# Spread LayerNorm rows, one product for places and slot weights, ScalarE roots, banks per half: one block of retention, convolution and 32 experts

## The chip, the cores and the metric

The kernel runs on one core of one Trainium2 chip. The metric is the device time of one execution in microseconds (us). TensorE is written PE, VectorE DVE, ScalarE ACT, GpSimd POOL and SyncE, which here does nothing but issue DMAs, SP. Work reaches PE as matrix products in four-pass float32 (f32), in the rounded one-pass type fp32r, or in bf16.

## The reference

One post-norm layer over 256 tokens of width 1024 with a context prefix of 256 rows. A projection feeds two branches: retention with 8 heads (two heads make a pair p = 0..3 in the kernel) and a convolution with its own LayerNorm. Two sigmoid gates join them; a product with `w_mix_out`, a residual and LayerNorm 1 follow. Then each token goes to two of 32 experts, and LayerNorm 2 ends the layer. Every expert's weights are read, whatever the router chose.

```python
ret = jax.nn.silu(g) * _head_norm(o_ret)            # per head: (o - mean) * rsqrt(var + eps)
y_a = ret @ p['w_ret_out']
z = jax.nn.silu(_layernorm(_depthwise_conv(za * jax.nn.sigmoid(zb), ...), ...))
y_b = z @ p['w_conv_out'] + p['b_conv_out']
mix = (ga * y_a + gb * y_b) @ p['w_mix_out'] + p['b_mix_out']
h_lat = _layernorm(ALPHA * h_lat + gt_m * mix, p['ln1_g'], p['ln1_b'])
...
for e in range(N_EXPERTS):
    h = jax.nn.silu(t @ p['w_exp_gate'][e]) * (t @ p['w_exp_up'][e])
    y = y + combine[:, e:e + 1] * (h @ p['w_exp_down'][e])
h_lat = _layernorm(ALPHA * h_lat + gt_f * moe, p['ln2_g'], p['ln2_b'])
```

## The kernel before

**Order.** The kernel is recorded in the order in which it stands: `step` and `run_steps` keep a list of steps of the mixing sub-layer, `weave` inserts side steps at numbered places (`NPOS`, `APOS`, `TPOS`, `QPOS`), and each engine executes its own instructions in that order. A semaphore wait blocks everything behind it on its engine's queue. Because a product in fp32r keeps fewer bits, weights are split before use: `Slice.emit` lets ACT write the rounded half (`q[:, 0]`, L162) and DVE the rest (`q[:, 1]`, L163); `mm3` (L94 to L96) makes three fp32r products from the halves. The names are `qg` (gates), `qro` (`w_ret_out`), `qco` (`w_conv_out`), `qm` (`w_mix_out`).

**Last head pair and convolution norm.** While PE works on the first gates (`gate`, `gt`), `retain(3)` makes the retention outputs. Its `post` takes mean and variance (L684, L686) and gets the head norm's inverse root by integer arithmetic and Newton steps on DVE (`rstd`, L113 to L119). In the same loop `conv_rstd` starts the convolution's inverse root on DVE and gives its three Newton steps, twelve operations of 128x256, to POOL (L821 to L824). `post2` (L697, L700) scales and gates the heads on DVE alone. `ret_t` transposes them (`rt`, then `rT`, split by ACT and DVE), and `ret_out(3)` multiplies by `qro` into `ya`. `conv_norm` halves the normalisation between DVE and POOL (L829).

**The gate rows.** The adaLN sums `secs` (L918) are stored by POOL to a scratch row `arow` in DRAM (`rows_sum`). `rows_load` reads it back, spread over all partitions, into `tmp` and `gtf` (`bcast`, L78). Those two reads are issued by SP, which also issues all weight loads (`load`, L72). `conv_out(4..7)` (`yb`) then use `wco` tiles.

**LayerNorm 1 and router.** `mix_q` accumulates `mx`: the last accumulation of the second token tile goes in two halves of 256 columns that share a bank. `router_fold`, `router_mm` (`plog`) and `rank` pick the experts; `keep_clock(KC..)` adds idle products `clk`.

**Experts.** A list `plan` names 192 weight tiles of 1 MiB, six for each expert. `load_to` gives tile i the buffer class `slots[i]`: cycles of 18 tiles (`full`) up to slot `NCYC`, then 16 (`cyc`), then 12. A load waits until the buffer's last user is done. For each pair e0 = 0, 2, .. 30, `expert_pair` runs gate and up products (`gu`, L1375), `scatter` of the pair before (`y`, L1416), transposes (`ht`), `place`, which makes the slot-to-token matrix with two products and the slot weights with two more (`st`, L1450, L1452), and the down products (`dn`, L1485).

**LayerNorm rows.** The scale and shift rows of LN1 and LN2 lie on one partition (`lnv`). They are spread over 128 partitions by a product with a column of ones, in f32, 512 columns each: for LN1 at the end of pair 24 (`l1r`, L1645, used by L1647 to L1651 to start `yacc`), for LN2 at the end of pair 28 (`l2r`, L1657), behind the `tc.If` (L1628) that catches an overfull expert.

Of the kernel before, what the change touches and what calls it, by code (L numbers as in the profile page):

```python
# [17 lines left out]
D = 1024  # L18
# [13 lines left out]
NPOS, APOS, TPOS, QPOS, AHEAD = 7, 9, 7, 5, ()  # L32
# [4 lines left out]
NCYC = 130  # L37
CTX = 0, 0, 5, 6, 2
LNS = 20, 26, 24, 28
KC0, KC1, KC2, KC3, KC4 = 0, 2, 3, 4, 4  # L40
# [4 lines left out]
def tile_block(ctx, tc, a, out):  # L45
# [31 lines left out]
    def bcast(dst, src, n):  # L77
        nc.sync.dma_start(dst, bass.AP(tensor=src.tensor, offset=src.offset, ap=[[0, P], [1, n]]))  # L78
# [575 lines left out]
    def retain(p):  # L654
        box = {}

        def mm(_):
# [6 lines left out]
            if p == 3:  # L664
                conv_var()

        def post():
# [3 lines left out]
            more = []  # L671
            if p == 3:
                more = conv_rstd()
                for j in AHEAD:
                    more.insert(j, next_slice)

            def fill(i):
                if more:
                    more.pop(0)()
                elif i >= 2 and i % 3 != 1:  # L680
                    pop_conv(1)
# [5 lines left out]
            rstd(rs, mv[:, :, 1], 4, f"hn{p}", fill)  # L687
            while more:
                fill(0)
            box["n"] = mv, rs  # L690

        def post2():
            sr, (mv, rs) = srs[p], box["n"]
            for i in range(4):
                hh, t = divmod(i, 2)
                o = sr[:, 1, t, hh * NT:(hh + 1) * NT]
                V.tensor_scalar(o, box[hh][:, t], mv[:, i, 0:1], rs[:, i:i + 1], op0=ALU.subtract, op1=ALU.mult)  # L697
# [10 lines left out]

    last = []
# [104 lines left out]

    def conv_rstd():
        crs, ve, t = row1("crs"), row1("crsv"), row1("crst")
        nbox["rs"] = crs

        def newton():
# [6 lines left out]
        return rstd_ops(crs, nbox["var"], ve, t, 1.0 / D)[0:2] + [newton]  # L826
# [179 lines left out]
    def load_piece(which, o, n):  # L1006
        for e, t in which:
            load(t.rearrange("p k f -> p (k f)")[:, o:o + n], a["w_down"][e, 1, :, o:o + n])

    def down_view(t, cb):  # L1010

        t = t.rearrange("p k f -> p (k f)")
        return t.rearrange("p (k q f) -> p k q f", k=4, q=2) if cb == 0 else t.rearrange("p (q k f) -> p k q f", q=2, k=4)

    def load_to(n):
        while len(wts) < min(n, len(plan)):
# [5 lines left out]
            else:  # L1022
# [8 lines left out]
                t = down_view(t, r)  # L1031
# [6 lines left out]
    for p in range(3):  # L1038
# [10 lines left out]
          call(1, scores, 6), call(2, scores, 7), call(4, lambda: last.append(retain(3))), call(QPOS, step, lambda _: last[0]()),  # L1049
# [30 lines left out]
    def mix_q(cb, kq, box):  # L1080
        def mm(q):
            yT = ybox["y"]
            if kq == 0:
                box["ps"] = [acc(f"mx{cb}_{t}") for t in range(2)]
            box[kq] = q
            whole = slice(0, 512)
            order = [(kq, 0, whole), (kq, 1, whole)]
            if cb == 1 and kq >= 2:

                order = [(kq, 0, whole)]  # L1090
                if kq == 3:
                    order += [(n, 1, slice(256 * q, 256 * q + 256)) for q in range(2) for n in (2, 3)]
            for n, t, c in order:
                for kk in range(2):
                    k = 2 * n + kk
                    mm3(box["ps"][t][:, c], (yT[0][:, k, t * P:(t + 1) * P], yT[1][:, k, t * P:(t + 1) * P]),
                        (box[n][0][:, kk, c], box[n][1][:, kk, c]), k == 0, k == 7 and c.stop == 512)

        def post():
            if kq == 3:  # L1100
                r_ = [sb.tile([P, 512], F32, tag="b2", name=f"r{cb}_{t}", bufs=2) for t in range(2)]
                for t in range(2):
                    for q in range(2) if t and cb else (None,):
                        c = slice(0, 512) if q is None else slice(256 * q, 256 * q + 256)
                        cs = slice(512 * cb + c.start, 512 * cb + c.stop)
                        V.tensor_mul(r_[t][:, c], box["ps"][t][:, c], tmp[:, 1, cs])
                        V.tensor_add(xr[:, t, cs], xr[:, t, cs], r_[t][:, c])
                    for q in range(2):
# [649 lines left out]
```

## Time and profile before

| | us |
|---|---|
| median of 3 runs (974.23 to 975.60) | 975.26 |
| the profiled execution | 975.05 |
| its span on the core | 973.0 |
| PE busy | 928.3 (95%) |
| DVE busy | 518.5 (53%) |
| ACT busy | 313.2 (32%) |
| POOL busy | 100.6 (10%) |
| mean granted TensorE clock | 0.984 |

2.05 us of the profiled execution lie outside the span. The page gives shares over the whole span; the stages differ. Up to about 487 us PE works on the mixing sub-layer, from 500 us on the experts, and the last 13 us are LayerNorm 2. DMA moves 292.8 MB from HBM, two thirds of it expert weights. In a timeline row stand the start, the duration, engine, line, operation, out<-in, and in brackets the idle time ahead with the instruction that ended it. Successive products overlap, so the distance between two starts, not the duration, is the pace.

### The profile page before, as it was taken

What the parts mean: (1) busy time and instruction counts of PE and PEld (TensorE: products, weight loads), DVE (VectorE), ACT (ScalarE), POOL (GpSimd) and SP (SyncE); (2) the same over time, 40 slices, a digit from 0 to 9 for tenths busy, and PEclk for the clock granted to TensorE, in tenths of its full rate; (3) what the DMA queues carried; (4) which work ended last, traced back from release to release, by engine and by line L of the source; (5) the groups of instructions that cost most, each with busy time, mean ns of one, the idle gap of its engine ahead of it and who ended that gap; (6) DMA issues with size and microseconds to landing.
All of it is one profiled execution on the core that took longest, in us unless ns stands there. A gap on an engine that the chain in (4) does not pass through costs nothing. (4 is left out here: it accounts for less than half of the span.)

```text
span 973.0 us, 15303 instructions
## 1 busy us (share of the span) xinstructions
PE 928.3 (95%) x6327; PEld 688.2 (71%) x6327; DVE 518.5 (53%) x1000; ACT 313.2 (32%) x459; POOL 100.6 (10%) x114
## 2 busy tenths in 40 slices
PE   8999999999999999898999999999999999999994
PEld 6898798888789888798877656665555555535552
DVE  3598979878978976874844213121222222142126
ACT  2468444445345343653433102121111111112110
POOL 1020400400300213504100000000000000000001
PEclk9999999999999999999999999999999999989987
DMA  9967225634255176548998999999999999999971
GB/s 352 419 234 252 83 93 194 256 141 184 114 205 224 44 303 228 206 155 313 369 366 314 423 421 421 420 420 421 420 420 422 420 420 420 420 421 420 419 302 44
DMA packets 48744, 294.92 MB, mean 303 GB/s; under 512 B 10304, under 2 KB 10352, under 8 KB 14368
## 3 DMA queue, kind: packets, MB, share of 16 engines
q1 hardware_dynamic: 47888, 293.22, 75.3%
q8 instruction: 51, 0.84, 0.3%
q0 software_dynamic: 784, 0.70, 0.3%
q14 instruction: 21, 0.17, 0.0%
HBM read 292.77 MB, written 1.12 MB: 302 GB/s over the span
## 5 line engine op out<-in xcount | busy, mean ns | idle before, releaser
L1375 PE MATMUL gu<-wgate,xe 128*64 128x256 f32 x1024 | 123.0, 391 | 0.7 <-DMA wgate<-in_w_exp_gate_dram 0.5
L1375 PE MATMUL gu<-wup,xe 128*64 128x256 f32 x1024 | 117.7, 380 | 3.4 <-DMA wup<-in_w_exp_up_dram 3.4
L1485 PE MATMUL dn<-wdown,hT 128*64 128x512 f32 (+1 forms) x528 | 117.1, 583 | 3.6 <-DVE hT L1443 2.5
L335 DVE SCALAR_TENSOR_TENSOR slab<-zp,taps,slab 128x256 f32<-128x256 f32 x232 | 109.2, 525 | 0.0
L1375 PEld LDWEIGHTS gu<-wgate,xe 128*64 128x64 f32 x1024 | 74.6, 140 | 45.3 <-issue 9.9
L1381 DVE TENSOR_TENSOR h<-h,gu 128x256 f32<-128x256 f32 x32 | 13.5, 421 | 171.9 <-ACT h L1380 171.9
L1375 PEld LDWEIGHTS gu<-wup,xe 128*64 128x64 f32 x1024 | 73.9, 137 | 41.6 <-DMA wup<-in_w_exp_up_dram 6.6
L1485 PEld LDWEIGHTS dn<-wdown,hT 128*64 128x64 f32 x528 | 40.3, 137 | 68.2 <-issue 58.6
L1380 ACT ACTIVATE h<-gu 128x256 f32<-128x256 f32 x32 | 12.3, 384 | 205.5 <-PE gu L1375 205.5
L1498 DVE SCALAR_TENSOR_TENSOR dl<-dn,ws,ohq 128x512 fp32r<-128x512 f32 x30 | 22.5, 751 | 94.0 <-ACT ohq L1497 94.0
L1497 ACT ACTIVATE ohq<-dn,ws 128x512 fp32r<-128x512 f32 x30 | 20.6, 687 | 130.1 <-PE dn L1485 127.4
L1355 PEld LDWEIGHTS ga<-ohq,xh 128*128 128x128 f32 x224 | 27.9, 188 | 15.9 <-issue 11.1
L95 PE MATMUL ya<-rT,qro 128*128 128x256 f32 x128 | 36.7, 287 | 2.5 <-DVE rT L726 2.5
L75 POOL DMA_DIRECT2D lnv<-in_ln_g_dram x2 | 1.0, 521 | 367.3 <-PE dn L1485 302.8
L96 PE MATMUL glu<-ulh,qz 128*128 128x256 f32 x128 | 36.4, 284 | 1.9 <-DVE qz L163 1.9
L96 PE MATMUL gt<-ulh,qg 128*128 128x256 f32 x128 | 36.2, 283 | 1.9 <-DVE qg L163 1.9
L94 PE MATMUL glu<-ulh,qz 128*128 128x256 f32 x128 | 37.2, 291 | 0.2 <-ACT qz L162 0.2
L96 PE MATMUL ya<-rT,qro 128*128 128x256 f32 x128 | 36.6, 286 | 0.8 <-DVE qro L163 0.8
L1362 DVE TENSOR_SCALAR xe<-ga,cf 128x256 f32<-128x256 f32 x32 | 17.4, 544 | 37.2 <-ACT xe L1365 36.3
L94 PE MATMUL ya<-rT,qro 128*128 128x256 f32 x128 | 37.0, 289 | 0.0
L1355 PE MATMUL ga<-ohq,xh 128*128 128x256 f32 x224 | 33.6, 293 | 3.4 <-DVE dl L1498 3.4
L94 PE MATMUL gt<-ulh,qg 128*128 128x256 f32 x128 | 36.7, 287 | 0.0
(461 smaller groups left out, 2151.4 us busy)
## 6 DMA issues: line engine op xcount, KB each, us to landing
wgate<-in_w_exp_gate_dram SPq DMA_DIRECT2D x64, 1024.0 KB, 19.8
wup<-in_w_exp_up_dram SPq DMA_DIRECT2D x64, 1024.0 KB, 19.8
wdown<-in_w_down_dram SPq DMA_DIRECT2D x62, 1024.0 KB, 19.8
wa<-in_w_ada_r_dram SPq DMA_DIRECT2D x16, 1024.0 KB, 4.9
wa<-in_w_ada_m_dram SPq DMA_DIRECT2D x8, 1024.0 KB, 14.5
wro<-in_w_ret_out_dram SPq DMA_DIRECT2D x8, 1024.0 KB, 6.9
wg<-in_w_gates_dram SPq DMA_DIRECT2D x8, 1024.0 KB, 7.2
wz<-in_w_glu_dram SPq DMA_DIRECT2D x5, 1024.0 KB, 13.1
```

The source lines that it names most:

```text
L94: T.matmul(ps, st[0], mv[0], start=start, stop=False)
L95: T.matmul(ps, st[0], mv[1], start=False, stop=False)
L96: T.matmul(ps, st[1], mv[0], start=False, stop=stop)
L335: V.scalar_tensor_tensor(dst, zp[:, ct, j:j + NT], taps[:, ct, j:j + 1], ac[ct], op0=ALU.mult, op1=ALU.add)
L1355: T.matmul(ps[:, kk], halves[k // 4][:, s, t, P * (k % 4):P * (k % 4) + P], ohr[:, t], start=(t == 0 and s == 0), stop=(t == 1 and s == 1))
L1362: V.tensor_scalar(xe[c][:, k], ps[:, kk], fsc[:, k:k + 1], fsh[:, k:k + 1], op0=ALU.mult, op1=ALU.add)
L1375: T.matmul(ps[64 * hf:64 * hf + 64, j], xe[c][:, k, CAP * i:CAP * i + CAP], w[:, k % 4, NT * hf:NT * hf + NT], start=start, stop=stop)
L1380: S.activation(h, ps[:, 0], AF.Silu)
L1381: V.tensor_mul(h, h, ps[:, 1])
L1485: T.matmul(ps[64 * x:64 * x + 64], hT[x][:, ch % 2, 64 * (ch // 2):64 * (ch // 2) + 64], w, start=(ch == 0), stop=(ch == 3))
L1497: S.activation(dh, ps, AF.Copy, scale=ws)
L1498: V.scalar_tensor_tensor(dl, ps, ws, dh.bitcast(F32), op0=ALU.mult, op1=ALU.subtract)
```

## The change

1. **Rows.** `l1r` and `l2r` go. `pieces(n)` makes eight pieces of 256 columns of a LayerNorm's two rows; for each, ACT rounds the row piece and DVE takes the rest, and two fp32r products spread both halves into one bank. `row()` runs one piece after each `hidden` and after each half of the down products: LN1's in pairs 20 and 22, LN2's in pairs 24 and 26. `lnv` is loaded at the end of pair 18, `yacc` begins there too, and `NCYC` falls from 130 to 112.
2. **Places.** `iw` holds the identity and, beside it, the slot weights of all experts. Two products of 192 columns replace the two of 128 and two of 4; DVE then adds the pair's weights out of the bank.
3. **Roots.** For the last head pair and the convolution, ACT's square root and DVE's reciprocal with one Newton step replace integer start and Newton steps (`rstd_pair`, `conv_root`, `conv_rstd`). `post2` follows at once, with two of its four scalings on ACT (in all pairs), and `ret_t` moves one place ahead.
4. **Banks.** The two halves of the last `mx` get a bank each.
5. **Reads of `arow`** are issued by POOL instead of SP.
6. **Small.** `least` is made in `router_fold`; `og` goes to POOL, and `ig4` no longer needs it; the `KC` counts fall; the last two experts' down weights get a DRAM array of their own.

```diff
-NPOS, APOS, TPOS, QPOS, AHEAD = 7, 9, 7, 5, ()
+NPOS, APOS, TPOS = 7, 9, 6
-NCYC = 130
+NCYC = 112
-LNS = 20, 26, 24, 28
-KC0, KC1, KC2, KC3, KC4 = 0, 2, 3, 4, 4
+LNS = 18, 20, 22, 24
+KC0, KC1, KC2, KC3, KC4 = 0, 0, 2, 2, 3
...
+                rstd_pair(rs, mv[:, :, 1], "hn3", 4, conv_root)
+            V.scalar_tensor_tensor(nb, mv[:, :, 0], -1.0, rs, op0=ALU.mult, op1=ALU.mult)
+            box["n"] = mv, rs, nb
+            if p == 3:
+                post2()
+                conv_rstd()
...
+            for i in (1, 0, 3, 2):
+                if t:
+                    S.activation(o, box[hh][:, t], AF.Identity, scale=rs[:, i:i + 1], bias=nb[:, i:i + 1])
...
     def conv_rstd():
-            for _ in range(3):
-                G.tensor_mul(t, crs, crs)
-                G.tensor_mul(t, t, ve)
-                G.tensor_scalar(t, t, -0.5, 1.5, op0=ALU.mult, op1=ALU.add)
-                G.tensor_mul(crs, crs, t)
+        V.reciprocal(crs, crs)
+        V.tensor_mul(t, crs, crs)
+        V.tensor_mul(t, t, nbox["h"])
+        V.scalar_tensor_tensor(crs, t, 1.5, crs, op0=ALU.add, op1=ALU.mult)
...
-        bcast(tmp[:, 1], arow[0], D)
-        bcast(gtf, arow[1], D)
+        bcast(tmp[:, 1], arow[0], D, nc.gpsimd)
+        bcast(gtf, arow[1], D, nc.gpsimd)
...
-                box["ps"] = [acc(f"mx{cb}_{t}") for t in range(2)]
+                box["ps"] = [(t, c, n, acc(f"mx{cb}_{t}_{c}")) for t in range(2)
+                             for c, n in (((0, 256), (256, 256)) if t and cb else ((0, 512),))]
...
-                T.matmul(pt[:, t * P:(t + 1) * P], oh[t], identr, start=True, stop=True)
-            for t in range(2):
-                T.matmul(pt[:, NT:NT + 4], oh[t], Wr[:, t, e0 // 2], start=(t == 0), stop=(t == 1))
+                T.matmul(pw[:, t], oh[t], iw[:, t], start=True, stop=True)
...
+    def pieces(n):
+        def split(i, c):
+            row = lnv[0:1, i, 256 * c:256 * c + 256]
+            h = box["h"] = sb.tile([P, 2, 256], F32R, tag="rope", name=f"lnh{n}{i}{c}", bufs=1)
+            S.activation(h[0:1, 0], row, AF.Copy)
+            V.tensor_sub(h[0:1, 1], row, h[0:1, 0].bitcast(F32))
+        def use(i, c):
+            ps = bank("mi", f"ln{n}{i}{c}")[:, 0:256]
+            for j in range(2):
+                T.matmul(ps, oner[0:1], box["h"][0:1, j], start=(j == 0), stop=(j == 1))
+            if n:
+                S.activation(lnv[:, i, cs], ps, AF.Copy)
+                return
...
-        if e0 == LNS[3]:
-            for i in range(4):
-                ps = bank("mi", f"l2r{i}")
-                cs = slice(512 * (i % 2), 512 * (i % 2) + 512)
-                T.matmul(ps, onef[0:1], lnv[0:1, i // 2, cs], start=True, stop=True)
-                S.activation(lnv[:, i // 2, cs], ps, AF.Copy)
+        for n in range(2):
+            if e0 == LNS[2 * n]:
+                rows.extend(pieces(n))
+                rows.pop(0)()
```

SP's queue before the second half of the gates' end, at the reads of `arow` (`wco` and `wm` are tiles of `w_conv_out` and `w_mix_out`; `wgate` is an expert's). Before:

```order
L78 DMA tmp<-in_b_mix_out_dram 128x1024
L78 DMA tmp<-arow 128x1024
L78 DMA gtf<-arow 128x1024
L72 DMA wco_4326<-in_w_conv_out_dram 128x2048
L72 DMA wco_4387<-in_w_conv_out_dram 128x2048
L72 DMA wgate_0_4452<-in_w_exp_gate_dram 128x2048
L72 DMA wm_0_4454<-in_w_mix_out_dram 128x2048
```

The same place after; the two reads now stand on POOL's queue, behind the stores of `arow` and ahead of a product of gate and `yaT`.

```order
L78 DMA tmp<-in_b_mix_out_dram 128x1024
L72 DMA wco_4324<-in_w_conv_out_dram 128x2048
L72 DMA wco_4385<-in_w_conv_out_dram 128x2048
L72 DMA wgate_0_4450<-in_w_exp_gate_dram 128x2048
L72 DMA wm_0_4452<-in_w_mix_out_dram 128x2048
```

No weight load stands behind a read of `arow` any more. DVE in the stage of the last head pair, from the last small Newton operation on (`sr` are the scaled heads, `crs` the convolution's inverse root, `rT` the rest of the transposed heads). Before:

```order
L119 SCALAR_TENSOR_TENSOR rs_3645<-hn3t,rs_3645 128x4
L163 TENSOR_TENSOR qg_2_3686<-wg_1_3684,qg_2_3686 128x1024
L697 TENSOR_SCALAR sr_3336<-o_3623,mv_3644,rs_3645 128x256 x2
L697 TENSOR_SCALAR sr_3336<-o_3632,mv_3644,rs_3645 128x256 x2
L700 TENSOR_TENSOR sr_3336<-sr_3336 128x2x256 x2
L163 TENSOR_TENSOR qg_3_3722<-wg_1_3684,qg_3_3722 128x1024
L163 TENSOR_TENSOR qro_0_3753<-wro_0_3751,qro_0_3753 128x1024
L726 TENSOR_TENSOR rT_3782<-rt_0_3783,rT_3782 128x512
L829 TENSOR_TENSOR zp<-zp,crs 128x4x256
```

And after:

```order
L686 SCALAR_TENSOR_TENSOR nb_3651<-mv_3649,rs_3650 128x4
L700 TENSOR_SCALAR sr_3338<-o_3625,mv_3649,rs_3650 128x256
L700 TENSOR_SCALAR sr_3338<-o_3634,mv_3649,rs_3650 128x256
L703 TENSOR_TENSOR sr_3338<-sr_3338 128x2x256 x2
L824 RECIPROCAL crs<-crs 128x256
L825 TENSOR_TENSOR crst<-crs 128x256
L826 TENSOR_TENSOR crst<-crst,crsh 128x256
L827 SCALAR_TENSOR_TENSOR crs<-crst,crs 128x256
L165 TENSOR_TENSOR qg_2_3690<-wg_1_3688,qg_2_3690 128x1024
L165 TENSOR_TENSOR qg_3_3720<-wg_1_3688,qg_3_3720 128x1024
L727 TENSOR_TENSOR rT_3749<-rt_0_3750,rT_3749 128x512
```

The split of `qg_2` for the third pair of gates now stands behind the scaled heads and the whole inverse root; two scalings have left DVE. PE behind pair 28, where the `tc.If` ends. Before:

```order
L1628 UNCONDITIONAL_BRANCH
L1657 MATMUL l2r_7667<-lnv,oner 128x512
L1657 MATMUL l2r_7670<-lnv,oner 128x512
L1657 MATMUL l2r_7673<-lnv,oner 128x512
L1657 MATMUL l2r_7676<-lnv,oner 128x512
L1375 MATMUL gu_7679<-wgate_0_7358,xe_7181 64x256 x8
```

And after, and in a second fence where such products now stand (`ln`, between the experts of pair 20):

```order
L1682 UNCONDITIONAL_BRANCH
L1381 MATMUL gu_7750<-wgate_0_7445,xe_7245 64x256 x8
L1381 MATMUL gu_7750<-wgate_1_7447,xe_7245 64x256 x8
```

```order
L1381 MATMUL gu_6658<-wup_0_6439,xe_6458 64x256 x8
L1381 MATMUL gu_6658<-wup_1_6441,xe_6458 64x256 x8
L1642 MATMUL ln_6694<-lnh_6645,oner 128x256 x2
L1381 MATMUL gu_6702<-wgate_0_6443,xe_6458 64x256 x8
L1381 MATMUL gu_6702<-wgate_1_6445,xe_6458 64x256 x8
```

One piece of a row, two short products, follows the gate and up products of each expert, and the last pair's products follow the branch directly.

## Rows read from the trace of the kernel before

**Rows 1.** Windows: from:to, length, busy per engine, PEclk, DMA share, GB/s
```profile
404.00:407.00 3.00, 3.00 (x20) 3.00 (x19) 0.51 (x2) 0.67 (x3) 0.00 (x0) 0.66 0.81 330
435.00:440.00 5.00, 5.00 (x45) 5.00 (x44) 2.25 (x5) 2.84 (x4) 0.84 (x2) 1.00 0.00 0
525.00:530.00 5.00, 5.00 (x26) 2.89 (x24) 0.75 (x1) 0.69 (x1) 0.00 (x0) 1.00 0.31 128
900.00:925.00 25.00, 23.01 (x155) 12.74 (x152) 3.85 (x9) 2.85 (x6) 0.00 (x0) 1.00 1.01 419
```
**Rows 2.** DMA issues of the page: KB each, median us to landing
```profile
wgate<-in_w_exp_gate_dram SPq DMA_DIRECT2D x64, 1024.0 KB, 19.8
```
**Rows 3.** Waits of PE, 780 to 860 us: total, times, longest
```profile
PE gu L1375 <- DMA wup<-in_w_exp_up_dram: 3.4, 7, 0.7
```
**Rows 4.** Waits of SP's queue, 440 to 560 us
```profile
SPq L78 <- DMA arow<-secs: 19.2, 2, 18.9
SPq L72 <- PE dn L1485: 18.8, 3, 9.0
```
**Rows 5.** Timeline of SP, 420 to 456 us
```profile
441.19 0.33 SPq L78 DMA_DIRECT2D tmp<-arow  x1
...
442.37 0.86 SPq L72 DMA_DIRECT2D wco<-in_w_conv_out_dram  x2
```
**Rows 6.** Timeline of PE at the second half of the convolution's output
```profile
452.45 0.39 PE L94 MATMUL yb<-zh,qco 128*128 128x256 f32 x1 [2.63 <-ACT qco L162]
...
453.71 0.50 PE L96 MATMUL yb<-zh,qco 128*128 128x256 f32 x1 [0.76 <-DVE qco L163]
...
457.36 0.28 PE L95 MATMUL yb<-zl,qco 128*128 128x256 f32 x1
457.48 0.28 PE L96 MATMUL yb<-zh,qco 128*128 128x256 f32 x1
```
**Rows 7.** Timeline of PE, last head pair, 388 to 416 us
```profile
391.17 0.39 PE L96 MATMUL gt<-ulh,qg 128*128 128x256 f32 x1 [0.26 <-DVE qg L163]
...
396.30 0.39 PE L96 MATMUL gt<-ulh,qg 128*128 128x256 f32 x1 [1.60 <-DVE qg L163]
...
403.22 0.58 PE L95 MATMUL ya<-rT,qro 128*128 128x256 f32 x1 [2.54 <-DVE rT L726]
```
**Rows 8.** Timeline of DVE in the same stage
```profile
385.27 0.36 DVE L686 BATCH_NORM_AGGREGATE mv<-st 128x2 f32<-128x6 f32 x4
...
391.03 1.89 DVE L697 TENSOR_SCALAR sr<-o,mv,rs 128x256 f32<-128x256 f32 x4
392.85 1.73 DVE L700 TENSOR_TENSOR sr<-sr 128x512 f32<-128x512 f32 x2
...
403.09 1.21 DVE L163 TENSOR_TENSOR qro<-wro,qro 128x1024 fp32r<-128x1024 f32 x1
```
**Rows 9.** Reciprocals of DVE by form: busy us, mean ns
```profile
L254 DVE RECIPROCAL l<-l 128x16 f32<-128x16 f32 x1 | 0.3, 253 | 0.0
...
L1220 DVE RECIPROCAL dv<-dv 128x2 f32<-128x2 f32 x1 | 0.2, 166 | 0.1
```
**Rows 10.** Timeline of DVE at the last product of the mixing
```profile
490.25 0.42 DVE L1106 TENSOR_TENSOR r<-mx,tmp 128x256 f32<-128x256 f32 x1 [0.60 <-PE mx L96]
```
**Rows 11.** Timeline of PE, ends of pairs 24 and 28 and the last pair
```profile
865.42 6.04 PE L1375 MATMUL gu<-wgate,xe 128*64 128x256 f32 x32
871.30 3.62 PE L1375 MATMUL gu<-wup,xe 128*64 128x256 f32 x32
...
922.90 5.40 PE L1657 MATMUL l2r<-lnv,oner 1*128 1x512 f32 x8 [1.81 <-DVEq L1628]
928.24 5.36 PE L1375 MATMUL gu<-wgate,xe 128*64 128x256 f32 x32
...
948.45 5.96 PE L1485 MATMUL dn<-wdown,hT 128*64 128x512 f32 x32
```
**Rows 12.** Timeline of SP, 915 to 946 us: the last six loads
```profile
917.68 12.79 SPq L72 DMA_DIRECT2D wdown<-in_w_down_dram  x6
```

More of the change, by code (lines that the diff above doesn't have):

```diff
@@ L670, in post @@
             rs = sb.tile([P, 4], F32, tag="rs", name=f"rs{p}", bufs=2)
[L671 to L675, printed above, removed]
+            nb = sb.tile([P, 4], F32, tag="nb", name=f"nb{p}", bufs=1)
             def fill(i):
-                if more:
-                    more.pop(0)()
-                elif i >= 2 and i % 3 != 1:
+                if i >= 2 and i % 3 != 1:
                     pop_conv(1)
@@ L1007, in load_piece @@
         for e, t in which:
[L1008 to L1013, printed above, removed]
+            load(t.rearrange("p k f -> p (k f)")[:, o:o + n], a["w_down_last"][e - (NE - 2), :, o:o + n])
     def load_to(n):
@@ L1101, in post @@
                 r_ = [sb.tile([P, 512], F32, tag="b2", name=f"r{cb}_{t}", bufs=2) for t in range(2)]
-                for t in range(2):
[L1103 to L1108, printed above, removed]
-                        V.bn_stats(st1[:, t, 2 * cb + q], xr[:, t, 512 * cb + 256 * q:512 * cb + 256 * q + 256])
+                for t, c, w, ps in box["ps"]:
+                    cs = slice(512 * cb + c, 512 * cb + c + w)
+                    V.tensor_mul(r_[t][:, c:c + w], ps[:, 0:w], tmp[:, 1, cs])
+                    V.tensor_add(xr[:, t, cs], xr[:, t, cs], r_[t][:, c:c + w])
+                    if c or w == 512:
+                        for q in (2 * cb, 2 * cb + 1):
+                            V.bn_stats(st1[:, t, q], xr[:, t, 256 * q:256 * q + 256])
         key = (cb, kq // 2)
@@ L1482, in product @@
                 for x in range(2):
-                    w = wts[e0 + x, "down", cb][:, ch]
-                    w = w[:, cs.start // 256] if cs.stop - cs.start == 256 else w
+                    w = wts[e0 + x, "down", cb]
+                    w = w[:, cs.start // 256, ch] if last and cb else w[:, ch]
                     T.matmul(ps[64 * x:64 * x + 64], hT[x][:, ch % 2, 64 * (ch // 2):64 * (ch // 2) + 64],
@@ L1617, in tile_block, with one_, go, row @@
     lnv = yacc = None
+    def pieces(n):
+        box = {}
+        def split(i, c):
[4 more added lines that the diff above has]
+        def use(i, c):
+            cs = slice(256 * c, 256 * c + 256)
+            ps = bank("mi", f"ln{n}{i}{c}")[:, 0:256]
[4 more added lines that the diff above has]
+                return
+            r, o = divmod(c, 2)
+            for t in range(2):
+                if i == 0:
+                    V.scalar_tensor_tensor(yacc[:, t, cs].rearrange("p (q k) -> p k q", k=4),
+                                           ps.rearrange("p (q k) -> p k q", k=4), ALPHA,
+                                           xn[:, t, r, :, 64 * o:64 * o + 64], op0=ALU.mult, op1=ALU.mult)
+                else:
+                    V.scalar_tensor_tensor(yacc[:, t, cs], ps, ALPHA, yacc[:, t, cs], op0=ALU.mult, op1=ALU.add)
+        todo = [(i, c) for i in range(2) for c in range(4)]
+        def one_(j):
+            def go():
+                if j:
+                    use(*todo[j - 1])
+                if j < len(todo):
+                    split(*todo[j])
+            return go
+        return [one_(j) for j in range(len(todo) + 1)]
+    def row():
+        if rows:
+            rows.pop(0)()
+    rows = []
     for e0 in range(0, NE, 2):
```

115 lines of the change are left out of this document (58 added, 57 removed).

## The prediction

> **What bounds the kernel now.** I read the page's shares first, then windows of each stage, then the waits ahead of PE and of SP's queue, and the timelines where they stand. The page says PE is busy 95% of the span, which would make PE the bound everywhere. The windows say otherwise. In the expert stage the DMA share is 1.01 at 419 GB/s and PE has two us of 25 to spare [rows 1]; the 25 us windows from 550 to 925 all show 1.01 or 1.02. A tile of 1 MiB takes 1.0486 MB / 420 GB/s = 2.5 us, a pair of experts 12 x 2.5 = 30 us. PE needs 23.01 / 25 x 30 = 27.6 us for it, so it has about 2.4 us a pair, and from 780 us on it waits for weights, in short pieces [rows 3]. There the kernel ends when the weight stream ends, plus what PE does behind the last tile. PE is the bound in two places only: ahead of the stream, and behind it.
>
> The stream does not start by itself. At 525 to 530 us the DMA share is 0.31 [rows 1], and SP waits 18.8 us in three waits for PE's first down products, which hold the buffers [rows 4]. So whatever brings PE sooner to the experts moves the whole stream by as much, and whatever makes PE faster inside it is worth nothing. That is the frame for each part.
>
> **Reads of `arow` (b).** SP waits 18.9 us for `arow` [rows 4] and issues its read at 441.19; behind it stand `wco` (issued 442.37 [rows 5]), an expert tile and `w_mix_out`. In 435 to 440 us no byte moves [rows 1]. PE then stands still for 2.63 us and again for 0.76 us, waiting for the halves of `wco`, and runs slowly for a while [rows 6]. From 452.45 - 2.63 = 449.82 to 457.36 it starts 19 products; at the pace of the last two rows, 0.12 us each, they are 2.3 us. Lost: 7.54 - 2.3 = 5.3 us. After the change SP goes on to `wco` at once. Its buffers come free as the gates' weights are split; I put the last of these splits at about 436 us, and two tiles need 5 us of the idle DMA, so they land some 9 us ahead of need. I take the whole 5.3; the lower end is 4, if the splits themselves on ACT and DVE are late. POOL waits for its own store instead, for a landing of perhaps 2 us; behind that stand the product with `yaT` and the one for `tmp`, needed only when the convolution output is done. Nothing else queues there.
>
> **Last head pair and roots (a).** Before, PE loses 0.26 + 1.60 + 2.54 us [rows 7], and then the granted clock is 0.66 in 404 to 407 us [rows 1]: at its lower level for 0.34 / 0.5 x 3 = 2 us, which costs 1.0. With the bit before 404, some 5.6 us. After, the split of `qg_2` stands behind more work on DVE. Means end at 385.27 + 0.36 = 385.6 [rows 8]; nine small operations, with ACT's roots between, take about 1.9; two scalings instead of four, half of 1.89 [rows 8], 0.95; the gating 1.73 [rows 8]: 390.2. Then the reciprocal of 128x256, which the trace does not have. The rows have 253 ns for 16 columns and 166 for two [rows 9], 6.2 ns for each more, so 166 + 254 x 6.2 = 1.74 us. Three operations of 128x256 at 0.42 [rows 10] and the split at 1.21 [rows 8] end at 394.4. PE is out of weights at 391.17 - 0.26 = 390.9 [rows 7]: a wait of 3.5 us, where before there were 0.26. Behind it the weights and transposes are ahead of PE, since the twelve POOL operations and ACT's late transposes are gone, and the waits of 1.60 and 2.54 fall away. The 2.54 us wait was followed by the lower clock and the one of 1.60 was not, so I charge the long one with 1.2 us more: 4.7 us in all, a gain of 0.9. Upper end 2.3, if the clock holds; lower end -1.6, if the wait for `rT` stays as well (4.7 + 2.5 against 5.6). The two table loads that ACT now needs lie in idle time of ACT ahead of the roots and behind them. The scalings given to ACT in the other pairs lie beside a PE that is busy, at nothing.
>
> A word on the reciprocal: the rows show 6.2 ns a column where the other small operations show far less. The Trainium skill, "VectorE: DVE Perf Modes", section "First, the fixed hardware budget", says that the reciprocal is an iterative divide with a repeat count of 8; if that is eight cycles of the 0.96 GHz clock that its "Specifications" give, an estimate by that page is 256 x 8 / 0.96 + 150 ns = 2.3 us. By it the sum below would be 0.5 us higher; the rows speak for the shorter price.
>
> **Banks, `og`, clock products (c).** DVE waits 0.60 us for the whole last `mx`, though its first half is done by then [rows 10]: with its own bank that goes. `og` on POOL takes one operation of about 0.2 (the size of the small one in [rows 9]) off DVE's chain to the router, and the fewer idle products let the last `plog` start some 0.25 sooner. Sum 1.0; ends 0.3 (another wait is behind each) and 1.5.
>
> **Up to the stream:** 5.3 + 0.9 + 1.0 = 7.2 us, carried to the end by the frame above.
>
> **Inside the stream.** A piece is two products of 256 columns, 0.24 us at the pace of [rows 6]; four a pair are 1.0 us of the 2.4 spare. Its split needs ACT and DVE for one-partition operations, both idle there. `yacc` takes over the buffer of a weight tile and may hold DVE until PE has used that tile, which delays the down products of one pair by 1 us at most: in the spare time too. The places' product, two of 192 columns for two of 128 and two of 4, is nothing either way. The ring shrinks earlier (16 tiles instead of 18 from slot 112): with 19.8 us from issue to landing [rows 2], 8 tiles are under way, so PE may be 8 tiles, 20 us, late before a load is held up. I price the whole at 0; without the cover it would be 16 x 0.24 = 4 us.
>
> **Behind the stream (d).** Before, the LN2 rows take 5.40 us between the last pairs, and the products behind them run at 5.36 us instead of 3.62 [rows 11]: 7.1 us on the path to the last down products at 948.45. The LN1 rows cost PE the like (6.04 against 3.62, [rows 11]), which it carries as lateness into the last pairs. After, neither stands there. PE alone would reach the down products 7.1 us sooner or more. The stream allows more: the last six loads start at 917.68 [rows 12], so the first lands at 937.5, the second at 940.0, and four half tiles of 1.25 us by 945.0; the down products need the second, 8.4 us sooner than now. I take 7.5. Lower end 5.5, if PE has to wait for that tile and drops its clock (1.74, the difference above); upper end 8.4.
>
> **Sum.** 975.05 - 7.2 - 7.5 = 960.35 for the profiled execution; the span is 973.0, and the 2.05 us around it stay. The median of the runs lies 0.2 above that execution: **960.5**. By the ends of the terms: 975.25 - (4 - 1.6 + 0.3 + 5.5) = 967 to 975.25 - (5.3 + 2.3 + 1.5 + 8.4) = 957.7.
>
> **The rivals.**
> *The stream is not moved.* If DMA itself, not PE, is late between 441 and 525 us, the 7.2 us do not arrive; only the tail is gained: 975.25 - 7.5 = 967.7. Against it: the idle DMA at 435 to 440 and 525 to 530 [rows 1], together some 8 us.
> *The path does not open.* `wco` waits for its buffers instead of `arow`, or POOL's read lands late: b falls to about 1 and the time is 965.
> *The pieces cost clock (slower).* Both old row products, on one partition, had the clock fall behind them [rows 11]. If each of the 16 pieces did so at the 1.74 us of LN2, a pair of PE would take 4 x (0.24 + 1.74) = 7.9 us more with 2.4 to spare: late by 4 x 5.5 = 22 after pair 26, less 2 x 2.4 regained, 17 behind the stream where before it was 7.5; with 7.2 gained earlier, +2.5, and as the loads would then be held up too, some 979. It decides from about 1.5 us a piece. Against it: a piece is 0.24 us between full products, the old ones were 5 to 7 us in one stretch with waits.
> *Nothing measurable*, if two of these meet and the tail gives little: about 975.
>
> **How the numbers follow.** Forecast as worked out, 957 to 964.5: 0.62. Head stage or tail at its lower end, or `wco` late, 964.5 to 968: 0.15. Stream not moved, 967.7: 0.08. Better than 957, by waits that I don't see go: 0.07. Nothing: 0.03. Slower by the pieces: 0.05. A measurement of this kernel tells about 0.2%, 2 us, from no change. Faster 0.92, same 0.03, slower 0.05. The range 954 to 968 takes in the ends of the terms and the rival of the unmoved stream.
>
> **What would show it.** b: `wco` issued by 436 us, `yb` without a wait ahead, the DMA busy at 435 to 440. a: one wait of 3 to 4 us for `qg`, none for `rT`, a reciprocal of 1.7 us. c: the DVE wait for `mx` gone. Stream: DMA share 1.01 from about 523 us on. d: down products of the last pair at about 933 to 934 us (948.45 - 14.7), with wider gaps of PE at full clock in pairs 26 to 30. Wrong would be a clock under 1 in pairs 20 to 26, a DMA share under 1 after slot 112 (some 745 us), or a new wait of SP ahead of `wco`.

## The result and the profile after

| | before | after |
|---|---|---|
| median of 4 runs, us | 975.10 | 962.61 |
| lowest to highest, us | 974.23 to 975.60 | 961.64 to 963.80 |
| profiled execution, its span, us | 975.05, 973.0 | 962.05, 960.2 |
| mean granted TensorE clock | 0.984 | 0.991 |

After over before is 0.9873 (95% interval 0.9856 to 0.9891): 12.5 us less, where 960.5 us, 14.8 less, was forecast and 954 to 968 was the range. Time and range were right, but the terms were not, and two of their misses cancel.

To see where the time went I compare the starts of the same PE product in both traces.

| PE reaches | before | after | gained by then |
|---|---|---|---|
| a product of `qp`, after the decay rates | 89.38 | 90.54 | -1.2 |
| the `yb` product that waits for `zl`, after the roots | 417.73 | 418.31 | -0.6 |
| the 19th `yb` product of the second half | 457.21 | 452.38 | 4.8 |
| `ppos`, the router's end | 498.41 | 493.34 | 5.1 |
| first `gu` of the experts | 503.35 | 500.07 | 3.3 |
| places of pair 0 | 521.43 | 518.14 | 3.3 |
| places of pair 18 | 761.19 | 757.95 | 3.2 |
| last `y` ahead of the last half tiles | 954.34 | 941.85 | 12.5 |

The reads of `arow` gave what was forecast. SP's timeline after: `wco` no longer waits behind them; what holds it now are its buffers, and it is issued 15 us earlier ([rows 5] had it at 442.37).

```profile
422.23 0.38 SPq L78 DMA_DIRECT2D tmp<-in_b_mix_out_dram  x1
427.33 7.60 SPq L72 DMA_DIRECT2D wco<-in_w_conv_out_dram  x2
435.03 0.39 SPq L72 DMA_DIRECT2D wgate<-in_w_exp_gate_dram  x1
```

POOL's timeline after (start, duration):

```profile
446.51 0.57 POOL L78 DMA_DIRECT2D tmp<-arow  x1 [5.19 <-ACT qco L164]
447.07 0.56 POOL L78 DMA_DIRECT2D gtf<-arow  x1
```

POOL waits 5.2 us ahead of the reads. The bracket names a piece of `qco` on ACT, but what takes so long are POOL's own stores of `arow`: in the traces of five runs below the bracket in this place names them. The DMA issues, before and then after (KB each, median us from issue to landing), show that they land much later now that weights move at the same time. Only POOL's own product for `tmp` waits for the reads, 0.5 us.

```profile
arow<-secs POOLq DMA_DIRECT2D x2, 4.0 KB, 2.0
```

```profile
arow<-secs POOLq DMA_DIRECT2D x2, 4.0 KB, 5.8
```

Windows after (columns as in [rows 1]): 5 us that moved no byte now move 328 GB/s; the old row with clock 0.66 is whole; but around 494 us the granted clock has fallen to 0.50, the lower level of 1.2 GHz; in pairs 22 and 24 it stays at 1.00.

```profile
404.00:407.00 3.00, 3.00 (x28) 3.00 (x27) 2.02 (x3) 2.94 (x4) 0.00 (x0) 1.00 1.00 358
435.00:440.00 5.00, 5.00 (x45) 5.00 (x44) 2.80 (x4) 2.34 (x4) 0.25 (x1) 1.00 0.87 328
494.00:498.00 4.00, 3.90 (x11) 2.97 (x11) 0.50 (x3) 1.51 (x2) 0.00 (x0) 0.50 1.01 424
800.00:825.00 25.00, 23.51 (x170) 14.21 (x168) 9.78 (x23) 4.66 (x9) 0.48 (x1) 1.00 1.01 421
825.00:850.00 25.00, 23.51 (x182) 14.84 (x178) 5.99 (x15) 4.25 (x10) 0.00 (x0) 1.00 1.01 421
```

Two windows of the kernel before: the stretch that the one at 494 us is to be compared with, in which the clock was 1.00, and one of the first half of the experts.

```profile
498.00:502.00 4.00, 3.48 (x22) 3.06 (x22) 1.21 (x5) 2.55 (x3) 0.00 (x0) 1.00 1.01 424
575.00:600.00 25.00, 24.82 (x188) 14.78 (x187) 6.26 (x13) 3.69 (x7) 0.00 (x0) 1.00 1.01 420
```

PE's timeline after. Waits of 3.16 and 1.06 us stand where [rows 7] had three and `zl` took 0.21; one of 1.19 at 90.54 is new; the second half of `yb` starts without one ([rows 6] had 2.63 and 0.76); the first gather of rows (`ga`) takes 5.42 us, where before it took 3.69 (the single row below); in the last pair no row products stand ahead of `gu` ([rows 11]).

```profile
90.54 0.39 PE L96 MATMUL qp<-ulh,qwq 128*128 128x256 f32 x1 [1.19 <-DVE qwq L165]
395.65 0.45 PE L96 MATMUL gt<-ulh,qg 128*128 128x256 f32 x1 [3.16 <-DVE qg L165]
418.31 0.39 PE L95 MATMUL yb<-zl,qco 128*128 128x256 f32 x1 [1.06 <-DVE zl L841]
450.25 0.28 PE L94 MATMUL yb<-zh,qco 128*128 128x256 f32 x1
493.34 0.19 PE L1288 MATMUL ppos<-M,tri 128*128 128x32 bf16 x1 [0.86 <-DVE M L1257]
494.72 5.42 PE L1364 MATMUL ga<-ohr,xn 128*128 128x256 f32 x16
917.00 3.67 PE L1381 MATMUL gu<-wgate,xe 128*64 128x256 f32 x32 [1.80 <-DVEq L1682]
935.38 6.53 PE L1493 MATMUL dn<-wdown,hT 128*64 128x512 f32 x32
941.85 1.98 PE L1535 MATMUL y<-ds,sT 128*128 128x512 f32 x4
```

```profile
499.73 3.69 PE L1358 MATMUL ga<-ohr,xn 128*128 128x256 f32 x16
```

DVE's timeline after: the reciprocal takes what was worked out; the 0.60 us ahead of the `r` of [rows 10] are gone, but at 488.95 DVE waits 0.81 us for ACT's root.

```profile
391.33 1.75 DVE L824 RECIPROCAL crs<-crs 128x256 f32<-128x256 f32 x1
394.38 4.35 DVE L165 TENSOR_TENSOR qg<-wg,qg 128x1024 fp32r<-128x1024 f32 x2
484.74 0.41 DVE L1102 TENSOR_TENSOR r<-mx,tmp 128x256 f32<-128x256 f32 x1
488.95 0.17 DVE L1221 RECIPROCAL dv<-dv 128x2 f32<-128x2 f32 x1 [0.81 <-ACT dv L1216]
```

### The profile page after: what moved, and what is told of

Read it like the earlier page. It is cut to its first block, busy times and chain, and to the rows that moved or that the text cites. A ratio compares the mean times of both kernels' runs of the same rounds, so it can differ in the third digit from the quotient of the medians.

```text
span 960.2 us, 15325 instructions
## 1 busy us (share of the span) xinstructions
PE 915.4 (95%) x6311; PEld 682.2 (71%) x6311; DVE 527.4 (55%) x1019; ACT 325.0 (34%) x492; POOL 95.8 (10%) x106
## 3 DMA queue, kind: packets, MB, share of 16 engines
q0 software_dynamic: 1072, 1.74, 0.6%
## 5 line engine op out<-in xcount | busy, mean ns | idle before, releaser
L1381 PE MATMUL gu<-wgate,xe 128*64 128x256 f32 x1024 | 117.7, 381 | 1.8 <-DVEq L1682 1.8
L335 DVE SCALAR_TENSOR_TENSOR slab<-zp,taps,slab 128x256 f32<-128x256 f32 x232 | 114.6, 546 | 0.0
L1381 PEld LDWEIGHTS gu<-wgate,xe 128*64 128x64 f32 x1024 | 72.4, 137 | 40.7 <-issue 2.8
L1361 PEld LDWEIGHTS ga<-ohq,xh 128*128 128x128 f32 x224 | 27.7, 188 | 14.8 <-issue 7.9
L96 PE MATMUL ya<-rT,qro 128*128 128x256 f32 x128 | 36.1, 282 | 0.8 <-DVE qro L165 0.8
L95 PE MATMUL gt<-ull,qg 128*128 128x256 f32 x128 | 36.6, 286 | 0.0
L94 PE MATMUL ya<-rT,qro 128*128 128x256 f32 x128 | 36.2, 283 | 0.0
L95 PE MATMUL glu<-ull,qz 128*128 128x256 f32 x128 | 36.1, 282 | 0.0
```

Source lines behind the costliest of these rows:

```text
L94: T.matmul(ps, st[0], mv[0], start=start, stop=False)
L95: T.matmul(ps, st[0], mv[1], start=False, stop=False)
L96: T.matmul(ps, st[1], mv[0], start=False, stop=stop)
L335: V.scalar_tensor_tensor(dst, zp[:, ct, j:j + NT], taps[:, ct, j:j + 1], ac[ct], op0=ALU.mult, op1=ALU.add)
L1361: T.matmul(ps[:, kk], halves[k // 4][:, s, t, P * (k % 4):P * (k % 4) + P], ohr[:, t], start=(t == 0 and s == 0), stop=(t == 1 and s == 1))
L1381: T.matmul(ps[64 * hf:64 * hf + 64, j], xe[c][:, k, CAP * i:CAP * i + CAP], w[:, k % 4, NT * hf:NT * hf + NT], start=start, stop=stop)
```

## The experiments

The theory after the result: the reads are worth 5.4 us, the row products 9 us by PE's own time, the roots next to nothing as they are ordered; and three places give gains back, the decay rates (1.0), the split of `qg_2` behind the reciprocal (3) and the fewer idle products ahead of the router (1.8). Places, banks and `og` have no run of their own; what is said of them comes from the traces. Rivals stand with the runs. Ratios are to the kernel before; after's is 0.9873.

**The reads back on SP.** After, with the two reads on SP's queue:

```diff
-        bcast(tmp[:, 1], arow[0], D, nc.gpsimd)
-        bcast(gtf, arow[1], D, nc.gpsimd)
+        bcast(tmp[:, 1], arow[0], D)
+        bcast(gtf, arow[1], D)
```

> The changed kernel (962.6 us) with the two reads of arow issued by SP again. Theory, the reads on SP blocked the loads of w_conv_out: SP waits some 18.9 us for arow again, no byte moves at 435 to 440 us, PE waits 2.6 + 0.8 us ahead of yb, and the time is 5.4 us longer, 968.0. Rival, the wait was closed by something else (earlier buffers, another order): the time stays within 1 us of 962.6.

970.29 us, ratio 0.9939 (0.9917 to 0.9961). SP's waits and the empty window are back as in [rows 4] and [rows 1]. The wait of SP's queue in this run (total, times, longest), the window, and PE's timeline at `yb`:

```profile
SPq L78 <- DMA arow<-secs: 19.4, 2, 19.1
```

```profile
435.00:440.00 5.00, 5.00 (x45) 5.00 (x44) 3.10 (x4) 2.22 (x3) 0.00 (x0) 1.00 0.00 0
```

```profile
454.45 0.58 PE L94 MATMUL yb<-zh,qco 128*128 128x256 f32 x1 [3.07 <-ACT qco L164]
```

By the traces PE is 7.6 us later at the experts, of which 1.2 come from the start of the program (last section): 6.4 us for the reads. The medians of the two kernels differ by 7.7, their ratios by 6.4.

**The reads alone**, in the kernel before (`bcast` takes the queue as an argument, as after):

```diff
-        bcast(tmp[:, 1], arow[0], D)
-        bcast(gtf, arow[1], D)
+        bcast(tmp[:, 1], arow[0], D, nc.gpsimd)
+        bcast(gtf, arow[1], D, nc.gpsimd)
```

> The kernel before with one part of the change: the two reads of arow issued by POOL. Theory, this part alone gives the 5.3 to 5.4 us of the prediction, and the weight stream carries them to the end: 975.4 - 5.4 = 970.0, no wait of PE at 449 to 454 us. Rival, without the rest of the change another wait stands there, or the stream is not moved: 973 or more.

969.01 us, 0.9935 (0.9917 to 0.9954): 6.4 less than before by the medians. By its trace PE is 7.1 us earlier at the experts: 5.4 come at `yb`, 0.4 from the start, and 1.2 from a clock that stayed up after a wait for `rT` of 2.56 us, after which it fell in the kernel before [rows 1, 7]; a window of this run:

```profile
403.00:407.00 4.00, 4.00 (x35) 4.00 (x36) 2.76 (x5) 2.88 (x6) 0.00 (x0) 1.00 0.82 293
```

Both ways b measures 5.4 to 6.4, and the rival that the stream would not be moved falls: 7.0 of the 7.1 us are there in pair 18, and 5.7 at the last down products. The rest is lost behind the old row products of this kernel, which take 6.15 us here and the products behind them 6.22, where [rows 11] have 5.40 and 5.36.

**The rows back in one stretch.** After, with the old `l1r` and `l2r`:

```diff
-NCYC = 112
+NCYC = 130
-LNS = 18, 20, 22, 24
+LNS = 20, 26, 24, 28
...
-        for n in range(2):
-            if e0 == LNS[2 * n]:
-                rows.extend(pieces(n))
-                rows.pop(0)()
...
+        if e0 == LNS[3]:
+            for i in range(4):
+                ps = bank("mi", f"l2r{i}")
+                cs = slice(512 * (i % 2), 512 * (i % 2) + 512)
+                T.matmul(ps, onef[0:1], lnv[0:1, i // 2, cs], start=True, stop=True)
+                S.activation(lnv[:, i // 2, cs], ps, AF.Copy)
```

> The changed kernel with the LayerNorm rows spread in one go as before (f32 products of 512 columns at the ends of pairs 24 and 28, ring of 18 tiles up to slot 130). Theory, the rows cost PE time at the end of a stream that DMA bounds, and the changed kernel's last down products came 9.2 us sooner than the earlier start of the stream alone explains: these 9 us come back, 971.5 to 972. My term in the prediction, 7.5 us: 970.1. Rival, the end is set by the landing of the last tiles and most of the gain came from their earlier issue: less than 5 us come back, under 967.5.

970.84 us, 0.9952 (0.9936 to 0.9968): 8.2 more than after by the medians, 7.7 by the ratios. The start is the same, the span of the profiled execution 8.9 us longer. PE's timeline of this run in the last pair:

```profile
919.51 5.56 PE L1663 MATMUL l2r<-lnv,oner 1*128 1x512 f32 x8 [1.81 <-DVEq L1634]
925.00 5.21 PE L1381 MATMUL gu<-wgate,xe 128*64 128x256 f32 x32
...
944.93 5.96 PE L1491 MATMUL dn<-wdown,hT 128*64 128x512 f32 x32
```

SP's timelines of the last loads, of after and then of this run:

```profile
914.01 2.85 SPq L72 DMA_DIRECT2D wdown<-in_w_down_dram  x2
919.09 7.75 SPq L72 DMA_DIRECT2D wdown<-in_w_down_last_dram  x4
```

```profile
914.29 2.62 SPq L72 DMA_DIRECT2D wdown<-in_w_down_dram  x2
919.02 7.77 SPq L72 DMA_DIRECT2D wdown<-in_w_down_last_dram  x4
```

The loads are issued within 0.3 us of each other: what the rows cost is PE's time behind the stream, not the stream's.

**The rows alone**, in the kernel before:

```diff
-NCYC = 130
+NCYC = 112
-LNS = 20, 26, 24, 28
+LNS = 18, 20, 22, 24
...
             hs.append(hidden(e0))
+            row()
...
+        for n in range(2):
+            if e0 == LNS[2 * n]:
+                rows.extend(pieces(n))
+                rows.pop(0)()
```

> The kernel before with the spread rows alone (pieces in pairs 20 to 26, ring of 16 tiles from slot 112). Theory, the last down products then wait for their tile and for nothing else, 9 us sooner than before: 966.4. By the prediction's term 7.5: 967.9. Rival, the gain needs the earlier stream as well: 970 or more.

965.11 us, 0.9895 (0.9851 to 0.9939): 10.3 less than before by the medians. The profiled execution is the slowest of four (968.63, the others 964.37 to 965.67). In it the experts start 2.5 us late, 2.1 of it because the granted clock stays lower for longer behind the waits for `rT` and ahead of `yb`, and the last `y` is 6.4 us early: 8.9 behind the stream, as in the run above. Two of PE's last down products go ahead, and the other 30 now wait for their second tile, in PE's timeline of this run:

```profile
942.67 5.34 PE L1487 MATMUL dn<-wdown,hT 128*64 128x512 f32 x30 [0.27 <-SPq L1676]
```

**Place or type of the pieces.** After, with one f32 product a piece instead of two of rounded halves:

```diff
-            h = box["h"] = sb.tile([P, 2, 256], F32R, tag="rope", name=f"lnh{n}{i}{c}", bufs=1)
-            S.activation(h[0:1, 0], row, AF.Copy)
-            V.tensor_sub(h[0:1, 1], row, h[0:1, 0].bitcast(F32))
+            box["h"] = row
...
-            for j in range(2):
-                T.matmul(ps, oner[0:1], box["h"][0:1, j], start=(j == 0), stop=(j == 1))
+            T.matmul(ps, onef[0:1], box["h"], start=True, stop=True)
```

> The changed kernel with each row piece spread by one f32 product of 256 columns straight from the row, without rounded half and rest. Theory, it is the place of the pieces that counts, between full products and beside spare time of PE, not their type: time within 1 us of 962.6, clock 1.00 in pairs 20 to 26. Rival, the f32 products on one partition make the clock fall as they did in one go: windows of pairs 20 to 26 under 1.00 and the time 5 us or more longer.

963.10 us, 0.9877 (0.9848 to 0.9905), no different from after. The groups of this run and then of after (busy, mean ns, idle ahead):

```profile
L1639 PE MATMUL ln<-lnv,oner 1*128 1x256 f32 x32 | 11.1, 426 | 0.0
```

```profile
L1642 PE MATMUL ln<-lnh,oner 1*128 1x256 f32 x32 | 8.2, 330 | 1.1 <-DVE lnh L1636 1.1
```

Even the dearer kind costs no clock (1.00 in 775 to 900 us in this run too): that the rows lie apart, among full products, is what counts; their halves are worth nothing here.

**The old roots.** After, with integer start and Newton steps on POOL, as before (`rstd` for head pair 3, `newton` in `conv_rstd`, four scalings on DVE):

```diff
-NPOS, APOS, TPOS = 7, 9, 6
+NPOS, APOS, TPOS, QPOS, AHEAD = 7, 9, 7, 5, ()
...
-            else:
-                rstd_pair(rs, mv[:, :, 1], "hn3", 4, conv_root)
...
+            rstd(rs, mv[:, :, 1], 4, f"hn{p}", fill)
...
```

> The changed kernel with the roots of the last heads and the convolution, the scalings and the place of the transposes as before. Theory by the traces, the stage from 385 to 418 us gained 0.6 us in all: 963.2. By the prediction's term 0.9: 963.5. Rival, the old order is as good or better, since the waits for qg, zl and the lower clock in 395 to 399 us are all new: 962 or less.

961.64 us, 0.9851 (0.9817 to 0.9885). The interval takes in after's ratio: the new roots are worth nothing that can be measured. PE's waits of this run, 385 to 425 us, and of after:

```profile
PE ya L95 <- DVE rT L726: 2.6, 1, 2.6
PE gt L96 <- DVE qg L165: 1.9, 2, 1.6
```

```profile
PE gt L96 <- DVE qg L165: 3.2, 1, 3.2
PE yb L95 <- DVE zl L841: 1.1, 1, 1.1
```

One set of waits took the place of the other. By the traces, counted from 91 us, after is 0.9 ahead at 418 us and not ahead at 500. The four runs lie in two pairs, at 959.3 to 959.4 and at 963.9 to 964.7 us, and the trace is of the second: whether the old roots are even a little better is open.

**The split first.** After, with the next slice of gate weights split ahead of the convolution's reciprocal:

```diff
                 post2()
+                next_slice()
                 conv_rstd()
```

> The changed kernel with the split of the third gate weights' first half ahead of the convolution's inverse root on DVE. Theory, PE's wait of 3.16 us at 395.65 comes from the reciprocal and its three operations standing ahead: the wait falls below 0.5 us, the convolution's activations on ACT come 1 us or more sooner too, since they stand behind the last gate's sigmoid, and the time is 1.5 to 3 us shorter, about 960.5. Rival, the convolution's norm becomes the late one: the wait ahead of yb for zl (1.06) grows by what the other one loses, and the time stays at 962.6 or grows.

958.08 us, 0.9810 (0.9783 to 0.9836): 4.5 less than after by the medians. DVE, then PE, in this run:

```profile
391.32 1.22 DVE L165 TENSOR_TENSOR qg<-wg,qg 128x1024 fp32r<-128x1024 f32 x1
392.46 1.74 DVE L825 RECIPROCAL crs<-crs 128x256 f32<-128x256 f32 x1
```

```profile
396.77 0.39 PE L96 MATMUL gt<-ulh,qg 128*128 128x256 f32 x1 [0.63 <-DVE qg L165]
```

The wait of 3.16 falls to 0.63, the clock in 390 to 400 us is 1.00 (after: 0.83), and the wait for `zl` stays (1.03). This run is 3.7 us ahead of after at 418 us and 3.5 at the experts.

**The idle products back.** After, with the old counts of products that only keep PE busy ahead of the router:

```diff
-KC0, KC1, KC2, KC3, KC4 = 0, 0, 2, 2, 3
+KC0, KC1, KC2, KC3, KC4 = 0, 2, 3, 4, 4
```

> The changed kernel with the old counts of idle products around the router (0, 2, 3, 4, 4). Theory, the fewer idle products let TensorE's clock fall at 491 us and the first gather ran at half rate (5.4 us for 16 products, 3.7 before): clock 1.00 from 490 to 502 us, first gather 3.7 us, time 1.8 us shorter, 960.8. Rival, the fall came from the wait for M (0.86 us) and not from their number: clock and gather as in the changed kernel, time 962.6 to 963.

961.66 us, 0.9846 (0.9818 to 0.9874). The medians don't part it from after. The trace does: from 91 to 500 us this run gains 1.9 us on after. Its window, and its first gather in PE's timeline:

```profile
494.00:498.00 4.00, 3.48 (x22) 3.06 (x22) 1.15 (x5) 2.72 (x4) 0.00 (x0) 1.00 1.01 422
```

```profile
495.74 3.69 PE L1364 MATMUL ga<-ohr,xn 128*128 128x256 f32 x16
```

All profiles agree on this. In the eight kernels with the low counts the first gather takes 4.03 to 5.56 us and the granted clock falls around it; in the five with the old counts it takes 3.69 and the clock stays at 1.00.

**The decay rates.** After the change two of their parts share one tile. First suspicion: the sharing ties them together. After, with two tiles:

```diff
-        l23 = row1("l23", (P, 2, 16))
-        l2, l3 = l23[:, 0], l23[:, 1]
+        l2, l3 = row1("l2", (P, 16)), row1("l3", (P, 16))
```

> The changed kernel with the decay rates' l2 and l3 in two tiles instead of one. Theory, sharing one tile makes ACT's second table load and logarithm wait for DVE's reciprocal, 1.06 us, and PE waits 1.19 us at 90.5: that wait goes, everything up to the end is 1.2 us sooner, 961.4. Rival, a later wait takes the 1.2 us up before the weight stream: 962.6.

963.22 us, 0.9866 (0.9842 to 0.9890), and ACT's wait is unchanged, so that suspicion fell. ACT's timeline of this run:

```profile
81.61 1.28 ACT L255 ACT_TABLE_LOAD   x1 [1.14 <-DVE l L253]
```

What remained, as a reading that this run does not show: the buffer has been used earlier in the program, so that the logarithm must wait for its own engine's earlier work and for DVE, and one of these waits stands on the table load ahead of it. What the traces show is that the load then starts when DVE is done, instead of beside DVE; before, it had no wait.

**The three mends together**: the split first, the idle products back, and the decay parts in a buffer that nothing has used.

The first two edits are those above; the third:

```diff
-        l23 = row1("l23", (P, 2, 16))
-        l2, l3 = l23[:, 0], l23[:, 1]
+        l23 = sb.tile([P, 2, 4, 6], F32, tag="st12", name="l23", bufs=1).rearrange("p t a b -> p t (a b)")
+        l2, l3 = l23[:, 0, 0:16], l23[:, 1, 0:16]
```

> The changed kernel with the split of the third gate weights ahead of the inverse root, the old counts of idle products, and the decay rates' two parts in a buffer that nothing else has used before them, so that ACT's logarithm waits for one engine and its table load for none. Theory, the three are on the path ahead of the weight stream and add up: 3.5 to 4.5 (first), 1.6 (second), 1.2 (third), so 955.5 to 956.5, with no wait of PE at 90 us. Rival, one of them is taken up by a wait behind it (for zl, or for the first weight tiles once PE is early): 958 or more.

**956.12 us, 0.9804 (0.9780 to 0.9828)**: 6.5 less than after and the fastest of all. ACT, then PE, in this run:

```profile
82.45 1.28 ACT L256 ACT_TABLE_LOAD   x1
```

```profile
491.63 3.69 PE L1365 MATMUL ga<-ohr,xn 128*128 128x256 f32 x16
```

The table load waits for nothing, PE no longer waits at 90 us, and 488 to 500 us run at clock 1.00. That the earlier tenants of the buffer make the load wait is shown as far as changing the buffer removes the wait. What this mend is worth by itself has no run.

**PE time inside the stream.** The frame of the prediction says that a faster PE is worth nothing there and that PE has some 2.4 us a pair to spare. After, with three idle products (six records in the trace) at each point at which a piece could stand and none does:

```diff
     def row():
         if rows:
             rows.pop(0)()
+        else:
+            keep_clock2(3)
```

> The changed kernel with idle products added in the expert pairs that have no row piece: three products of 128 columns in f32 after each expert and each half of the down products, some 0.5 to 0.6 us each time, about 2 us a pair, 20 us in all. Theory, the stage is bound by DMA and PE has some 2 us a pair to spare: the time stays within 1.5 us of 962.6, and PE's waits for weights get fewer. Rival, PE is the bound at least up to where it first waits for weights (some 780 us): 8 us longer or more.

994.76 us, 1.0199 (1.0153 to 1.0244). PE's timeline of this run, with one set and the places of pairs 8 and 10, and that of after with the same two pairs:

```profile
629.18 0.94 PE L1278 MATMUL clkq<-oner,ident 128*128 128x128 f32 x6
...
640.12 0.45 PE L1457 MATMUL st<-iw,ohq 128*128 128x192 f32 x2
...
670.09 0.45 PE L1457 MATMUL st<-iw,ohq 128*128 128x192 f32 x2
```

```profile
625.65 0.45 PE L1457 MATMUL st<-iw,ohq 128*128 128x192 f32 x2
...
651.81 0.45 PE L1457 MATMUL st<-iw,ohq 128*128 128x192 f32 x2
```

A pair takes 30.0 us here and 26.2 to 26.9 in after, whose DMA share is 1.01 there; here it is 0.95 between the two rows of places, and SP's loads wait 199 us in all for `gu` products to free buffers, where they wait 67 in after. Some 3.4 us in each of nine pairs make most of the 32; with 2.4 us to spare it would have been 1 us a pair. The frame, as put, is wrong, and the kernel before already showed it: the 2.4 us were read from 900 to 925 us, where PE is busy 23.01 of 25, but from 550 to 775 us it is busy 24.3 to 24.8 (one such window stands in the section on the result). What holds is narrower: up to pair 18 PE does not wait for weights but works off tiles that already lie in the buffers. It gains some 3.4 us a pair on the 30 us that a pair's weights take, until it first waits for a weight tile, at 784 us in the kernel before. By the traces PE time from there on is free only as far as it takes the place of such waits; in after the pieces take it, and the first wait for a tile stands at 869 us.

## Why the prediction was right, and where it was not

**b, reads of `arow`.** Right in size and cause: 5.3 forecast, 5.4 in the trace, 6.4 and 5.4 in the traces of the two runs that isolate it. `wco` does wait for its buffers, as a rival had it, but so early that the path opens. POOL's own wait was mis-sized, as its stores land after 5.8 us and not after the 2 that held before, and harmless as argued.

**a, roots.** 0.9 forecast, 0.6 in the trace, nothing in the comparison of times. The wait for `qg` was placed well (3.5 against 3.16), and the reciprocal was 1.74 against 1.75. (The term's upper end should read 2.1, which is 5.6 less 3.5, and not 2.3.) The Trainium skill, "VectorE: DVE Perf Modes", section "First, the fixed hardware budget", gave with its repeat count of 8 an estimate of 2.3; the 1.75 of the trace does not bear eight cycles out. The failed sentence is "the waits of 1.60 and 2.54 fall away": they did, but 1.06 for `zl` came in behind them, and the low clock after the wait lasted to 399 us: 0.83 over 390 to 400 us makes 3.4 us at the lower level and 1.7 lost, where 1.2 were charged. I also took the order for given: with the split ahead of the reciprocal the same stage is 3.7 us shorter.

**c, banks, `og`, idle products.** 1.0 forecast. Up to `ppos` 0.2 came, as the 0.60 us saved at the bank are taken by 0.81 us for ACT's root. Then 1.8 were lost. The step that failed is the smallest of that paragraph: I counted the removed idle products as 0.25 us gained and did not ask what they were there for. Without them the clock falls.

**Decay rates.** The prediction doesn't name them. They cost 1.0 us, by a wait of 1.19 that the order of instructions does not show.

**Up to the stream** this makes 3.3 instead of 7.2, with -0.1 from the start: 5.4 + 0.6 - 1.0 - 0.1 + 0.2 - 1.8 = 3.3. The 3.3 were kept unchanged from pair 0 to pair 18. "Carried to the end" held; the step that failed is its reason, that PE has 2.4 us a pair to spare all along the stream, as the run with idle products showed.

**Inside the stream.** Priced at 0, and by the traces it is 0 for the stream: clock 1.00, DMA share 1.01, and SP waits for buffers of `gu` and `dn` as long as before (105.4 us against 104.7 in 500 to 960 us). PE itself is delayed by 1.9 us from pair 18 to pair 20 (places at 787.25, before at 788.60, so that 1.35 of the 3.24 us are left), and for the stream that costs nothing: its last loads are issued 3.7 us earlier than before. The slower rival falls: neither kind of piece lowers the clock.

**d, behind the stream.** 7.5 forecast with 8.4 as upper end; 9.2 in the trace, 8.9 in the traces of both runs that isolate it (8.2 and 10.3 by the medians). The term that was too small is the stream's bound: I took 0.9 off for waiting; I compared the landing of the second tile with the start of the down products as a whole, but two of the 32 products go ahead of that tile (0.4); and the last loads are issued 3.7 us earlier (914.01 against 917.68 in [rows 12]) and not 3.3 (0.4). In after the down products start at 935.38 (933 to 934 was forecast), are drawn out to 6.53 us instead of 5.96 by the wait for that tile, and the next product starts 12.5 us earlier than before.

**Sum.** Forecast less found: b 0.1 too little, a 0.3 and c 2.6 too much, the decay rates 1.0 and the start 0.1 unseen, d 1.7 too little: 14.7 against 12.5 at the last `y`, 12.8 in the span. That the time came within 2.1 us of the forecast is in part luck, as d's error paid for a good part of c's; without it 964.3 us would still have been in the range.

## What to carry to other kernels

Ask of every small DMA that depends on computed data which loads stand behind it on its queue; moving two reads to another queue gave half of this gain. Put long products on few partitions in short pieces between full ones, well ahead of a stage's end. Before idle products are removed or a long DVE operation is put ahead of a weight split, look at what the next wait will be and at the clock behind it: one line of order, four numbers and another buffer were worth another 6.5 us here.

## What the runs showed of the hardware that was not expected

The first stretch of idle products, at 10.7 us, takes 1.60 us in 8 of the 13 profiles and 2.93 in 5 (or its records look so), and all that follows is some 1.2 us later, whatever the kernel. The runs with the idle products back, the old roots and the three mends were among the five. So single traces are compared here from a landmark behind it, and differences of 1 us between medians are left open.

After one and the same wait for `rT` of 2.5 to 2.6 us the clock fell in the kernel before and in the two runs with the old roots and the rows alone, and stayed at 1.00 in that with the reads alone. What decides between them is open; it is worth 1.2 us.

The second table load of the decay rates, 1.28 us on ACT, stands still for 1.06 to 1.14 us behind DVE in the nine kernels whose decay parts lie in a buffer with earlier tenants, and has no wait in the four others; it then no longer lies beside the work on DVE. How a wait gets onto the load is not shown.

The two stores of 4 KB into `arow` land 2.0 us after their issue (median of the two) in the three kernels with the reads on SP, where no weights move at that time, and 4.9 to 6.7 us after it in the ten with the reads on POOL, where they do.
